# Raw x for the last block's early u, position-major GLU columns, and S4 in the place of S1 with four ev buffers

## The chip, the cores and the metric

The kernel runs on one NeuronCore of a Trainium2 chip. The metric is the device time of one execution in microseconds (us); before the change the median of three runs is 2195.66 us (2195.51 to 2199.68). TensorE (PE) does the matrix products, VectorE (DVE) and ScalarE (ACT) the elementwise work, GpSimd (POOL) a few small powers and some transfers, SyncE (SP) issues most transfers.

## The reference

One decoder layer over 2064 tokens (16 meta tokens ahead of 2048) of width 1024, all in fp32:

```python
hn = rms_norm(h, norm_mix_g)
b_gate, c_gate, v, u = split(hn @ w_in, 4)                 # 512 columns each
conv_out = b_gate * causal_dwconv(c_gate * v, conv_w)
# s5_group_ssm: diagonal complex state space over all tokens, then
g = gelu(Re(C s) + D * u);  ssm_out = g * sigmoid(g @ w_glu)
h = h + concat(rms_norm(conv_out), rms_norm(ssm_out)) @ w_out
hn = rms_norm(h, norm_ffn_g)
a, val = split(causal_dwconv(hn @ w_up, ffn_conv_w, ffn_conv_b))   # 2816 each
h = h + (silu(a) * val) @ w_down
y = rms_norm(h, norm_final_g)[16:]
```

rms_norm multiplies a token by the inverse root mean square over its 1024 features and by a gain g per feature. The inverse root is one number per token, so it can also be multiplied onto a matrix product's output column.

## The kernel before, in words

Features lie on the 128 partitions and tokens along the free dimension. Six chunks of 344 tokens (numbered 0 to 5, q in the code) make three blocks of two chunks. Every fp32 operand is split in a high and a low part, hi = round(x) by ACT and lo = x - hi by DVE; a product is three matmuls with 344 columns, wh times xh, wh times xl, wl times xh. Names with h_ and wh_ are high parts, l_ and wl_ low ones. The weights of a product come by a transfer (wr_), then ACT forms wh_ and DVE wl_.

The stages, in order of time: u and the gated convolution of block 0 (u_block, conv_block; the coefficients of the state space are made on DVE at the same time); the early u of the last block, u_block(2), from about 157 us; u_block(1); conv_block 1 and 2 with the scan of the state space beside them, to about 485 us; the GLU, matmuls pg in glu_block from 505 to 572 us; output projections po to 745 us; then the MLP in three token blocks of some 480 us each. An up product of the MLP is made of two-by-two block products of the weights and of x: seven products (forms) in the place of eight, on sums S1 to S4 of weight blocks, formed on DVE, and on sums of x (t1 to t4 and b21, b22 in the names).

A program written in Python generates the instructions; a scheduler with costs of its own then fixes one order per engine, and each engine works through its order without skipping. Within that, generators (prep) hand out the preparing work of the next chunk in steps between matmul units, and Feed hands out weight splits of the MLP, up to four ahead of use, with three raw weight tiles (tag wr, 3 buffers) in flight.

What the change touches:

- prep_x, as used for chunks 4 and 5, loads the two halves of a chunk, 4 times 344 columns each (x_c), sums the squares (ACT L164 sq_c, DVE adds, PE st_c), forms the inverse root (DVE sv_c, POOL sr_c, DVE dg_c, PE sb_c, ACT rs_c), multiplies it and the gain onto x (DVE L241 t_c, four instructions a half), and only then splits (ACT h_c, DVE l_c). raw_x, used for chunks 0 and 1, splits x times gain at once (ACT L389, DVE L390) and leaves the inverse root to the outputs.
- The halves of x live in a pool with three buffers; a fourth half is loaded when the first has been read for the last time.
- u_block writes a product into ut, transposed to rows of eight positions j, and stores that to u_d (L893). With the inverse root still open this is a DVE multiply (block 0), else an ACT copy (L892).
- After the scan, gt holds g as 4 x 8 x 258 on each partition: feature group k, position j in a group of eight tokens, group c. prep_glu (L1021 and the subtraction behind it) writes gh and gl in token order, with stride 8 across j. glu_block multiplies sg, the sigmoid, onto gt and reads it with stride 8 (tokens()). prep_ssm (from L1033) does the same kind of split for the output projection.
- Pair and PairTile form the weight sums: job 0 splits the raw tile r0 as loaded, then forms three sums in place (S1 in r0's first half, one in its second half, one in the first half of the raw tile r1) and the fourth, S4, in a tile of its own, tag w4, in the pool fp; jobs 1, 2 and 3 split r0 with its sums, S4, and r1. self.freed says at which job a raw tile counts as free for the next load: jobs 1 and 3.
- ev2_tile, the outgoing buffers of the down products (ACT L1525 writes ev, POOL L1529 sends it), has three buffers.

## Time and profile before

| | |
|---|---|
| median of three runs | 2195.66 us (2195.51 to 2199.68) |
| profiled execution, its time | 2199.4 us |
| its span, first to last instruction | 2197.6 us |
| PE busy in the span | 2119.1 us (96%), 13012 matmuls |
| DVE, ACT, POOL busy | 1688.0, 1097.5, 153.2 us |
| mean granted TensorE clock | 0.984 |
| PE idle, 0 to 250 us / 500 to 800 us / 800 to 2197.6 us | 26.7 / 20.0 / 28.2 us |

The span is the stretch from the first to the last instruction of one execution; the profiled one is 3.7 us above the median of the runs. The last row is the window length less PE's busy time in the windows view. A matmul with 344 columns shows about 320 ns in the list, but the next starts while it drains: in stretches without waits one starts each 0.15 to 0.16 us. "Idle before <- X" on a row is the time that the engine stood still ahead of the instruction, and what released it. PEclk is the granted TensorE clock, 1.00 at full speed.

### The profile page before, as it was taken

How to read it: one execution, taken by the hardware profiler on the slowest of the kernel's cores; microseconds unless marked ns; L12 is line 12 of the kernel's file. 1: busy time of each engine (PE TensorE's matmuls, PEld its weight loads, DVE VectorE, ACT ScalarE, POOL GpSimd, SP SyncE). 2: the span in 40 equal slices, each digit the busy share in tenths (PEclk: the TensorE clock that was granted, in tenths of full speed). 3: DMA queues.
4: the chain of work that ended last, by engine and by line, in shares of the span. 5: the costliest groups of instructions: out<-in, count | busy, mean ns of one | idle time of the engine just before them, and what ended most of it. 6: DMA issues, size and time to landing. Idle time of an engine off the chain costs nothing.

```text
span 2197.6 us, 33162 instructions
## 1 busy us (share of the span) xinstructions
PE 2119.1 (96%) x13012; PEld 2057.7 (94%) x13012; DVE 1688.0 (77%) x2539; ACT 1097.5 (50%) x1651; POOL 153.2 (7%) x174
## 2 busy tenths in 40 slices
PE   8997999999899999999999999999999999999997
PEld 7997999998898999999999999999899999999996
DVE  8896498857866796886679878777768878767776
ACT  4135333236523365554556556555456556545555
POOL 0000000000000001101110010100111010110010
PEclk9998999999999999999999999999999999999999
DMA  7376544352475336635552554744554362654463
GB/s 246 104 219 169 142 144 146 116 169 74 144 232 187 100 98 158 157 90 122 133 127 76 144 119 122 184 103 130 147 136 109 103 166 82 163 118 99 98 168 118
DMA packets 170750, 300.29 MB, mean 137 GB/s; under 512 B 32416, under 2 KB 104800, under 8 KB 170464
## 3 DMA queue, kind: packets, MB, share of 16 engines
q1 hardware_dynamic: 149856, 246.41, 36.3%
q0 software_dynamic: 19584, 47.52, 13.0%
q10 hardware_dynamic: 1152, 4.23, 0.5%
q8 instruction: 102, 1.67, 0.3%
q14 instruction: 56, 0.46, 0.1%
HBM read 214.29 MB, written 83.82 MB: 136 GB/s over the span
## 4 chain that ended last, share of the span: by engine, by line
PE 60%; issue 8%; DVE 5%; ACT 3%; DMA 3%; POOL 1%; SPq 0%; POOLq 0%; DVEq 0%; ACTq 0%
PE xy L1427 9%; PE xy L1429 8%; PE xy L1428 8%; PE dn L138 6%; PE dn L139 6%; PE dn L142 6%; PE pz L1429 3%; PE pz L1427 3%; PE pz L1428 3%; PE po L138 2%; PE po L142 2%; PE po L139 1%; DMA v_b<-h_d 1%; DMA gt<-g_d 1%; ACT h_ms L1038 1%
## 5 line engine op out<-in xcount | busy, mean ns | idle before, releaser
L109 DVE TENSOR_TENSOR wl_up<-wr_up,wh_up 128x1024 fp32r<-128x1024 f32 x198 | 241.8, 1222 | 140.7 <-ACT wh_up L248 138.5
L138 PE MATMUL dn<-ah,wh_dn 128*128 128x344 f32 (+1 forms) x1024 | 327.8, 324 | 11.4 <-ACT ah L248 8.8
L139 PE MATMUL dn<-al,wh_dn 128*128 128x344 f32 (+1 forms) x1024 | 325.5, 321 | 0.4 <-DVE al L109 0.3
L248 ACT ACTIVATE wh_up<-wr_up 128x1024 fp32r<-128x1024 f32 x198 | 209.6, 1059 | 230.8 <-PE dn L139 56.4
L1427 PE MATMUL xy<-h_t,wh_up 128*128 128x344 f32 (+1 forms) x792 | 262.8, 332 | 0.0
L1429 PE MATMUL xy<-h_t,wl_up 128*128 128x344 f32 (+1 forms) x792 | 253.4, 320 | 0.0
L1428 PE MATMUL xy<-l_t,wh_up 128*128 128x344 f32 (+1 forms) x792 | 252.7, 319 | 0.0
L142 PE MATMUL dn<-ah,wl_dn 128*128 128x344 f32 (+1 forms) x1024 | 248.1, 321 | 0.0
L138 PEld LDWEIGHTS dn<-ah,wh_dn 128*128 128x128 f32 x1024 | 193.2, 189 | 17.1 <-ACT ah L248 9.7
L1529 POOL DMA_DIRECT2D h_d<-ev x136 | 118.3, 870 | 1261.8 <-ACT ev L1525 1251.4
L139 PEld LDWEIGHTS dn<-al,wh_dn 128*128 128x128 f32 x1024 | 194.2, 190 | 2.0 <-DVE al L109 1.2
L1427 PE MATMUL xy<-h_b,wh_up 128*128 128x344 f32 (+1 forms) x528 | 175.6, 334 | 6.1 <-ACT ev L1525 4.6
L142 PEld LDWEIGHTS dn<-ah,wl_dn 128*128 128x128 f32 x1024 | 178.4, 190 | 0.0
L1428 PE MATMUL xy<-l_b,wh_up 128*128 128x344 f32 (+1 forms) x528 | 169.0, 320 | 0.0
L1429 PE MATMUL xy<-h_b,wl_up 128*128 128x344 f32 (+1 forms) x528 | 167.6, 320 | 0.0
L1427 PEld LDWEIGHTS xy<-h_t,wh_up 128*128 128x128 f32 x792 | 149.2, 188 | 17.1 <-ACT z L1472 11.1
L248 ACT ACTIVATE wh_dn<-wr_dn 128x512 fp32r<-128x512 f32 (+1 forms) x144 | 85.5, 594 | 133.6 <-issue 56.7
L1428 PEld LDWEIGHTS xy<-l_t,wh_up 128*128 128x128 f32 x792 | 149.9, 189 | 0.0
L1429 PEld LDWEIGHTS xy<-h_t,wl_up 128*128 128x128 f32 x792 | 149.6, 189 | 0.0
L115 DVE SCALAR_TENSOR_TENSOR g<-z,pv,g 128x688 f32<-128x688 f32 (+1 forms) x132 | 122.3, 926 | 23.7 <-ACT g L1432 22.9
L115 DVE SCALAR_TENSOR_TENSOR v<-z,pneg,v 128x688 f32<-128x688 f32 (+1 forms) x132 | 122.4, 927 | 10.3 <-ACT v L1432 9.0
L109 DVE TENSOR_TENSOR wl_dn<-wr_dn,wh_dn 128x512 fp32r<-128x512 f32 (+1 forms) x144 | 92.3, 644 | 45.6 <-ACT wh_dn L248 44.9
(413 smaller groups left out, 5358.3 us busy)
## 6 DMA issues: line engine op xcount, KB each, us to landing
wr_up<-in_w_up SPq DMA_DIRECT2D x132, 512.0 KB, 5.0
h_d<-ev POOLq DMA_DIRECT2D x88, 344.0 KB, 6.6
wr_dn<-in_w_down SPq DMA_DIRECT2D x96, 256.0 KB, 2.6
wr_cw<-in_w_in SPq DMA_DIRECT2D x36, 512.0 KB, 4.6
h_d<-ev POOLq DMA_DIRECT2D x48, 336.0 KB, 6.7
x_c<-in_xq SPq DMA_DIRECT2D x16, 688.0 KB, 6.4
wr_dn<-in_w_down SPq DMA_DIRECT2D x48, 192.0 KB, 2.3
xr<-in_xq SPq DMA_DIRECT2D x24, 344.0 KB, 3.7
```

The source lines that it names most:

```text
L109: V.tensor_tensor(out, a, b, op=op)
L115: V.scalar_tensor_tensor(out=out, in0=a, scalar=s, in1=b, op0=ALU.mult, op1=ALU.add)
L138: T.matmul(ps[c], hi[:, k, :], xh, start=k == 0, stop=False)
L139: T.matmul(ps[c], hi[:, k, :], xl, start=False, stop=False)
L142: T.matmul(ps[c], lo[:, k, :], xh, start=False, stop=k == nk - 1)
L248: S.activation(hi, t, AF.Copy)
L1038: S.activation(tokens(hi), t, AF.Copy)
L1427: T.matmul(ps, hi[:, j, :], xh[:, j, :], start=start and j == 0, stop=False, **kw)
L1428: T.matmul(ps, hi[:, j, :], xl[:, j, :], start=False, stop=False, **kw)
L1429: T.matmul(ps, lo[:, j, :], xh[:, j, :], start=False, stop=j == 3, **kw)
L1529: G.dma_start(out=h_d[:, m, s0 : s0 + no], in_=ev, accum_op=ALU.add)
```

## The change

Three edits, and their names. First, chunks 4 and 5 go through raw_x for the early u of the last block: they are split without the inverse root, x of chunk 4 is loaded ahead of conv_block(0), the inverse root is kept in rs_2 (the same single buffer as that of block 0), and ut is then written by a DVE multiply. Second, prep_glu writes gh and gl by position (j c) and no longer by token, and glu_block reads sg in runs of 43. Third, in the MLP S4 is formed in the first half of r0, where S1 lay, after S1's split; r0 counts as free after job 2 instead of job 1; the tile w4 goes; ev2 gets a fourth buffer.

```diff
-    rs0 = rs_tile("rs0")[:, :, :QL]
+    rs_of = {}
-    def raw_x(q, res):
+    def raw_x(q, res, b, other=False, late=None):
         xs, out = [], []
+        kw = dict(pool=xf2, tag="xhl2", bufs=4) if other else {}
         for i in range(2):
             xs += load_halves((xq[q, :, 4 * i : 4 * i + 4, :],), QL, f"c{q}{i}")
             yield
-        for i, x in enumerate(xs):
-            hi, lo = hl_tile(QL, f"h_c{q}_{i}"), hl_tile(QL, f"l_c{q}_{i}")
+        def split_half(i, x):
+            hi, lo = hl_tile(QL, f"h_c{q}_{i}", **kw), hl_tile(QL, f"l_c{q}_{i}", **kw)
             for k in range(4):
                 g = col(C_MIX + 4 * i + k)
                 S.activation(hi[:, k, :], x[:, k, :], AF.Copy, scale=g)
...
-        yield from inv_rms(xs, QL, f"c{q}", rs0[:, q, :])
+        for i, x in enumerate(xs):
+            if late is None:
+                split_half(i, x)
+            else:
+                late.append(lambda x=x, i=i: split_half(i, x))
+            yield
+        if b not in rs_of:
+            rs_of[b] = rs_tile(f"rs_{b}")[:, :, :QL]
+        yield from inv_rms(xs, QL, f"c{q}", rs_of[b][:, q % 2, :])
...
-                prep.add(prep_x(4, hu, other=True), prep_x(5, hu, late=late))
+                prep.add(ahead[0], raw_x(5, hu, 2, late=late))
...
-            if b == 0:
-                mul(out, by_j(ps[:, :, :QL]), by_j(rs0))
+            if b in rs_of:
+                mul(out, by_j(ps[:, :, :QL]), by_j(rs_of[b]))
...
     u_block(0, hc[0])
+    ahead = [raw_x(4, hu, 2, other=True)]
+    next(ahead[0])
+    next(ahead[0])
     conv_block(0, hc[0], late_after=True, n_prep=4)
...
-            S.activation(tokens(hi), src, AF.Copy)
-            tt(tokens(lo), src, f32(tokens(hi)), ALU.subtract)
+            hj, lj = (a.rearrange("p k (j c) -> p k j c", j=NJ) for a in (hi, lo))
+            S.activation(hj, src, AF.Copy)
+            tt(lj, src, f32(hj), ALU.subtract)
...
-            g = gt[:, m, :, b * 86 : b * 86 + 86]
-            mul(g, g, tokens(sg))
+            g = gt[:, m, :, b * 86 : b * 86 + 86].rearrange("p j (c x) -> p c j x", c=2)
+            mul(g, g, two(sg).rearrange("p c (j x) -> p c j x", j=NJ))
...
-            self.freed = int(i in (1, 3))
+            self.freed = int(i > 1)
...
-                pair.s4 = fp.tile([P, 4, P], F32, tag="w4", bufs=1, name=f"w4_{pair.name}")
-                tt(pair.s4, r1[:, 4:8, :], b, ALU.add)
                 return w
-            return split_weights((r0, pair.s4, r1)[i - 1], 4 if i == 2 else 8, f"{pair.name}_{i}")
+            if i == 2:
+                return split_weights(a, 4, f"{pair.name}_2")
+            w = split_weights(r0 if i == 1 else r1, 8, f"{pair.name}_{i}")
+            if i == 1:
+                tt(a, r1[:, 4:8, :], b, ALU.add)
+            return w
...
-        return fp.tile([P, MAX_OUT], F32, tag="ev2", bufs=3, name=name)
+        return fp.tile([P, MAX_OUT], F32, tag="ev2", bufs=4, name=name)
```

The rows below are single instructions in the order in which an engine works through them: line, operation, output <- inputs with buffer numbers, columns on each partition, and xN for N like rows in a row. Line numbers are those of each version. In the GLU the order is the same in both; only the shapes differ.

DVE ahead of the early u of the last block (chunk 5: sv_c5 and dg_c5 are steps of its inverse root, t_c5 the normed x, l_c5 its low part, tab and wr, wi tables of the state space). Before:

```order
L198 TENSOR_SCALAR sv_c5_1652<-st_c5_1648 115x3
L109 TENSOR_TENSOR wi_0_2577<-tab_coarse_1320,tab_fine_1293 128x544
L203 TENSOR_SCALAR dg_c5_1656<-ident_75,sr_c5_1653 115x115 x2
L109 TENSOR_TENSOR st_0_2575<-wr_0_2576,wi_0_2577 128x544
L203 TENSOR_SCALAR dg_c5_1656<-ident_75,sr_c5_1653 115x115
L801 MEMSET sb_0_2755 128x4
L241 SCALAR_TENSOR_TENSOR t_c5_0_1729<-x_c5_0_1580,pv_84,rs_c5_1662 128x344 x4
L241 SCALAR_TENSOR_TENSOR t_c5_1_1734<-x_c5_1_1582,pv_84,rs_c5_1662 128x344 x4
L109 TENSOR_TENSOR l_c5_0_1795<-t_c5_0_1729,h_c5_0_1794 128x4x344
L109 TENSOR_TENSOR l_c5_1_1799<-t_c5_1_1734,h_c5_1_1798 128x4x344
```

Now, ending with the same sv_c5:

```order
L394 SCALAR_TENSOR_TENSOR l_c4_1_1428<-x_c41_0_659,pv_84,h_c4_1_1427 128x344 x4
L109 TENSOR_TENSOR tc_0_3_1725<-tc_0_3_1725,rs_0_184 128x688
L394 SCALAR_TENSOR_TENSOR l_c5_0_1786<-x_c50_0_1525,pv_84,h_c5_0_1785 128x344 x2
L109 TENSOR_TENSOR tc_0_3_1725<-cb_0_3_1730,tc_0_3_1725 128x688
L109 TENSOR_TENSOR wl_u22_1809<-wr_u22_1598,wh_u22_1808 128x1024
L109 TENSOR_TENSOR wl_u23_1886<-wr_u23_1670,wh_u23_1885 128x1024
L109 TENSOR_TENSOR sq_c5_0_1586<-sq_c5_0_1586,sq_c5_1_1588 128x4x344
L394 SCALAR_TENSOR_TENSOR l_c5_1_1796<-x_c51_0_1584,pv_84,h_c5_1_1795 128x344
L109 TENSOR_TENSOR sq_c5_0_1586<-sq_c5_0_1586 128x2x344
```

The low part of chunk 5 stood behind the inverse root of chunk 5 and now stands ahead of it.

DVE at the start of the MLP (up0_0 is the first pair of weight tiles; _2 is S4's split, _3 that of r1; po_2_7 is the last product of the output projection, xr its sum with x, l_b and l_t low parts of the MLP's x). Before:

```order
L109 TENSOR_TENSOR xr_2_7_6599<-po_2_7_6734,xr_2_7_6599 128x688
L109 TENSOR_TENSOR l_b22_0_6790<-v_b22_0_6585,h_b22_0_6789 128x4x338
L109 TENSOR_TENSOR l_b21_0_6794<-v_b21_0_6586,h_b21_0_6793 128x4x338
L109 TENSOR_TENSOR l_t3_0_6799<-v_b12_0_6584,h_t3_0_6798 128x4x338
L1217 TENSOR_SCALAR pneg_6814<-pv_84 128x22 x3
L109 TENSOR_TENSOR w4_up0_0_6829<-wr_up0_0_1_6820,wr_up0_0_0_6818 128x512
L109 TENSOR_TENSOR wl_up0_0_2_6836<-w4_up0_0_6829,wh_up0_0_2_6835 128x512
L109 TENSOR_TENSOR wl_up0_0_3_6840<-wr_up0_0_1_6820,wh_up0_0_3_6839 128x1024
```

Now:

```order
L109 TENSOR_TENSOR l_t4_0_6734<-v_b11_0_6586,h_t4_0_6733 128x4x338
L109 TENSOR_TENSOR wr_up0_0_0_6821<-wr_up0_0_1_6823,wr_up0_0_0_6821 128x512
L109 TENSOR_TENSOR wl_up0_0_2_6838<-wr_up0_0_0_6821,wh_up0_0_2_6837 128x512
L109 TENSOR_TENSOR xr_2_7_6602<-po_2_7_6737,xr_2_7_6602 128x688
L109 TENSOR_TENSOR l_b22_0_6793<-v_b22_0_6588,h_b22_0_6792 128x4x338
L109 TENSOR_TENSOR wl_up0_0_3_6842<-wr_up0_0_1_6823,wh_up0_0_3_6841 128x1024
L109 TENSOR_TENSOR l_b21_0_6797<-v_b21_0_6589,h_b21_0_6796 128x4x338
L109 TENSOR_TENSOR l_t3_0_6802<-v_b12_0_6587,h_t3_0_6801 128x4x338
```

S4's sum and split moved ahead of the last xr, and r1's split ahead of l_b21.

DVE at the change from the second to the third token block of the MLP (v_b11 to v_b22 are quarters of the next x, scaled by its inverse root rsk; up1_16 is a pair of weight tiles). Before:

```order
L1143 SCALAR_TENSOR_TENSOR v_b11_2_15387<-v_b11_2_15387,pv_84,rsk_2_13516 128x344 x2
L1143 SCALAR_TENSOR_TENSOR v_b21_2_15390<-v_b21_2_15390,pv_84,rsk_2_13516 128x344 x3
L109 TENSOR_TENSOR wl_up1_16_0_14829<-wr_up1_16_0_14715,wh_up1_16_0_14828 128x1024
L1143 SCALAR_TENSOR_TENSOR v_b12_2_15388<-v_b12_2_15388,pv_84,rsk_2_13516 128x344
L109 TENSOR_TENSOR wr_up1_16_0_14715<-wr_up1_16_0_14715,wr_up1_16_1_14762 128x512
```

Now:

```order
L1160 SCALAR_TENSOR_TENSOR v_b11_2_15349<-v_b11_2_15349,pv_84,rsk_2_13486 128x344 x3
L109 TENSOR_TENSOR wl_up1_16_0_14794<-wr_up1_16_0_14680,wh_up1_16_0_14793 128x1024
L1160 SCALAR_TENSOR_TENSOR v_b12_2_15350<-v_b12_2_15350,pv_84,rsk_2_13486 128x344
L109 TENSOR_TENSOR wr_up1_16_0_14680<-wr_up1_16_0_14680,wr_up1_16_1_14727 128x512
L1160 SCALAR_TENSOR_TENSOR v_b12_2_15350<-v_b12_2_15350,pv_84,rsk_2_13486 128x344
```

v_b21, the quarter that is loaded last, stood ahead of that pair's first split; now the first v_b21 stands thirteen rows behind it, ahead of S4's split.

More of the change, by code (lines that the diff above doesn't have):

```diff
@@ L384, in raw_x @@
             yield
-        for i, x in enumerate(xs):
-            hi, lo = hl_tile(QL, f"h_c{q}_{i}"), hl_tile(QL, f"l_c{q}_{i}")
+        if other:
+            kw["pool"] = xf2
+        def split_half(i, x):
+            hi, lo = hl_tile(QL, f"h_c{q}_{i}", **kw), hl_tile(QL, f"l_c{q}_{i}", **kw)
             for k in range(4):
@@ L393, in raw_x @@
             out.append((hi, lo))
+            if i == 1:
+                res.append(out)
+        for i, x in enumerate(xs):
[3 more added lines that the diff above has]
+                late.append(lambda x=x, i=i: split_half(i, x))
             yield
-        res.append(out)
-        yield from inv_rms(xs, QL, f"c{q}", rs0[:, q, :])
+        if b not in rs_of:
+            rs_of[b] = rs_tile(f"rs_{b}")[:, :, :QL]
+        yield from inv_rms(xs, QL, f"c{q}", rs_of[b][:, q % 2, :])
     sgn = col(C_SGN)
@@ L902, in conv_block @@
             if b == 0:
-                mul(two(vs), pv_[:, :, :QL], rs0)
+                mul(two(vs), pv_[:, :, :QL], rs_of[0])
             else:
@@ L910, in conv_block @@
             if b == 0:
-                mul(two(vs), two(vs), rs0)
+                mul(two(vs), two(vs), rs_of[0])
             tt(two(cv[:, 2:]), pc[:, :, :QL], two(vs), ALU.mult)
@@ L918, in conv_block @@
             if b == 0:
-                mul(two(tp), two(tp), rs0)
+                mul(two(tp), two(tp), rs_of[0])
             after_unit(n_prep=n_prep)
@@ L969, in layer_kernel @@
     hu, late = [], []
-    first = [raw_x(q, hc[0]) for q in range(2)]
+    first = [raw_x(q, hc[0], 0) for q in range(2)]
     next(first[0])
@@ L1320, in split @@
                 tt(b, b, a, ALU.add)
-                pair.s4 = fp.tile([P, 4, P], F32, tag="w4", bufs=1, name=f"w4_{pair.name}")
-                tt(pair.s4, r1[:, 4:8, :], b, ALU.add)
-                return w
-            return split_weights((r0, pair.s4, r1)[i - 1], 4 if i == 2 else 8, f"{pair.name}_{i}")
+                return w
+            if i == 2:
+                return split_weights(a, 4, f"{pair.name}_2")
+            w = split_weights(r0 if i == 1 else r1, 8, f"{pair.name}_{i}")
+            if i == 1:
+                tt(a, r1[:, 4:8, :], b, ALU.add)
+            return w
     jobs = []
```

## The prediction

> **What bounds the kernel now.** The page's first part and the windows view (columns: stretch, length, then busy time of each engine with its instructions in brackets, granted TensorE clock, DMA share, GB/s) come first.
>
> ```profile
> PE 2119.1 (96%) x13012; PEld 2057.7 (94%) x13012; DVE 1688.0 (77%) x2539; ACT 1097.5 (50%) x1651; POOL 153.2 (7%) x174
> 150.00:200.00 50.00, 38.90 (x224) 36.69 (x223) 37.95 (x55) 24.30 (x22) 2.04 (x2) 0.86 0.69 198
> 200.00:250.00 50.00, 46.47 (x292) 45.18 (x291) 20.05 (x27) 21.93 (x19) 1.50 (x2) 1.00 0.64 152
> 500.00:550.00 50.00, 45.10 (x254) 43.53 (x253) 43.21 (x50) 33.94 (x36) 3.20 (x3) 0.90 0.20 59
> 550.00:600.00 50.00, 44.35 (x264) 42.71 (x263) 44.01 (x62) 26.98 (x26) 3.10 (x3) 0.93 0.44 130
> 800.00:1050.00 250.00, 249.70 (x1581) 243.44 (x1581) 192.85 (x263) 136.94 (x219) 22.88 (x26) 1.00 0.50 124
> ```
>
> PE is busy 96% of the span, and no matmul is added or taken away, so only its waits and its half-clock stretches can be won. In 800 to 1050 us it is full: 250 us for 1581 matmuls, 0.158 us each. Counted so, 150 to 250 us holds 516 matmuls, 81.5 us of work, and 18.5 us are lost; 500 to 600 holds 518, 81.8 us, and 18.2 are lost. Those are the first two edits' stages. The third edit works in the MLP, where most windows are like the last row: there it can win little and lose much.
>
> **Part A, x of the last block without its inverse root.** The timeline of PE between 160 and 216 us shows the chain that u_block(2) waits for, then u_block(1); last the window with the half clock, and the DVE rows of the second chain.
>
> ```profile
> 164.82 0.76 PE L188 MATMUL st_c<-ones,sq_c 128*115 128x1 f32 x6 [3.33 <-DVE sq_c L109]
> 168.50 0.94 PE L208 MATMUL sb_c<-dg_c,ones 115*128 115x344 f32 x1 [2.92 <-DVE dg_c L203]
> 174.02 0.65 PE L138 MATMUL pu<-h_c,wh_u 128*128 128x344 f32 x1 [4.00 <-ACT h_c L248]
> 174.00:179.50 5.50, 4.63 (x15) 4.19 (x16) 4.08 (x5) 4.06 (x3) 0.00 (x0) 0.50 0.74 249
> 202.20 1.59 DVE L109 TENSOR_TENSOR sq_c<-sq_c,sq_c 128x1376 f32<-128x1376 f32 x1 [2.04 <-ACT sq_c L164]
> 213.48 3.10 DVE L109 TENSOR_TENSOR l_c<-t_c,h_c 128x1376 fp32r<-128x1376 f32 x2
> 215.12 0.43 PE L139 MATMUL pu<-l_c,wh_u 128*128 128x344 f32 x1 [1.34 <-DVE l_c L109]
> ```
>
> The edit takes the inverse root of chunks 4 and 5 off the path to their matmuls: these now need only the split. Removed on DVE are 16 t_c (L241) and four l_c of 1376 columns; added are 16 raw splits (L390's kind) and four ut multiplies in the place of ACT's copies. Per tile, DVE and ACT:
>
> ```profile
> L241 DVE SCALAR_TENSOR_TENSOR t_c<-x_c,pv,rs_c 128x344 f32<-128x344 f32 x48 | 24.0, 571 | 2.9 <-ACT rs_c L213 2.9
> L390 DVE SCALAR_TENSOR_TENSOR l_c<-x_c,pv,h_c 128x344 fp32r<-128x344 f32 x16 | 8.5, 572 | 5.9 <-ACT h_c L389 5.9
> L109 DVE TENSOR_TENSOR l_c<-t_c,h_c 128x1376 fp32r<-128x1376 f32 x12 | 18.7, 1589 | 0.0
> L109 DVE TENSOR_TENSOR ut<-pu,rs x4: 1450/1494/1534, 37.4 to 48.9; 128x688 f32<-128x688 f32 x4
> x_c<-in_xq SPq DMA_DIRECT2D x16, 688.0 KB, 6.4
> ```
>
> DVE does 16 x 0.57 + 4 x 1.59 = 15.5 us less and 16 x 0.57 + 4 x 1.49 = 15.1 more: nothing on balance; ACT gives up the four ut copies and forms h_c of chunks 4 and 5 in 16 pieces in the place of four, on an engine that is busy 24.30 and 21.93 us of 50 in the two windows above: nothing. What counts is the order. Followed by hand with these durations, PE goes on at once behind conv_block(0), where before it stood 3.33 + 2.92 + 4.00 us and ran at 0.50 until 179.5. One wait stays: the second half of chunk 5 gets its buffer only when chunk 4's first half is split, and the transfer takes 6.4 us; I get 2 us of PE idle (0 if it is issued early, 5 at twice the queue).
>
> That does not carry through to the end of u_block(1). Chunk 3's x is still normed first, and its second half needs a buffer that chunk 2's t_c gives back. The row at 202.20 starts its sum of squares and the one at 213.48 its low part: from 202.20 to the end of the first l_c, 213.48 + 1.55 = 215.0, are 12.8 us, a chain of DVE, PE, POOL and ACT that the edit leaves alone. In the new order t_c of chunk 2 comes about 6 us sooner, so this chain ends near 209, while PE would be there near 197. PE stands some 10 us in u_block(1), and the gain of about 19 us (the 18.5 lost plus rounding) shrinks to 215 - 209 = 6. From this I take 1 us for a half-clock stretch behind the new stand, as at 174 us. **A: 5 us won**; bounds 0 (chunk 3 no sooner than before) and 14 (its load lands early, and 18.5 less the waits left, 2 us and their half clock, is won).
>
> **Part B, the GLU's columns by position.** The view of tile gt (columns: minimum, median and maximum ns, first and last start), the group of the contiguous split of the conv half (l_mc), and the stage's PE rows:
>
> ```profile
> L109 DVE TENSOR_TENSOR gt<-gt,sg x12: 1395/1508/1556, 521.4 to 573.3; 128x688 f32<-128x688 f32 x12
> L1021 ACT ACTIVATE gh<-gt x6: 2768/2951/3092, 497.6 to 515.0; 128x1376 fp32r<-128x1376 f32 x6
> L109 DVE TENSOR_TENSOR gl<-gt,gh x6: 2754/2944/3064, 500.6 to 518.1; 128x1376 fp32r<-128x1376 f32 x6
> L164 ACT ACTIVATE sq_ms<-gt x6: 1355/1366/1382, 529.1 to 652.5; 128x1376 f32<-128x1376 f32 x6
> L109 DVE TENSOR_TENSOR l_mc<-t_mc,h_mc 128x1376 fp32r<-128x1376 f32 x6 | 9.4, 1590 | 0.1
> 562.01 0.86 DVE L109 TENSOR_TENSOR sq_mc<-sq_mc 128x688 f32<-128x688 f32 x1
> 507.51 0.65 PE L142 MATMUL pg<-gh,wl_g 128*128 128x344 f32 x1 [2.26 <-DVE wl_g L109]
> 534.60 0.42 PE L188 MATMUL st_ms<-ones,sq_ms 128*115 128x1 f32 x2 [1.79 <-DVE sq_ms L109]
> 564.04 0.32 PE L188 MATMUL st_mc<-ones,sq_mc 128*115 128x1 f32 x1 [4.87 <-DVE sq_mc L109]
> 534.50:542.00 7.50, 7.40 (x29) 7.43 (x30) 4.69 (x10) 0.76 (x1) 2.03 (x2) 0.54 0.26 72
> 504.80:564.00 59.20, 49.47 (x279) 47.61 (x278) 52.66 (x61) 39.91 (x40) 3.20 (x3) 0.90 0.18 51
> ```
>
> sq_ms reads gt in the same runs of 43 as gh and gl will, and takes 1.37 us; the strided writes take 2.95 for as many columns. So gh goes to 1.37, gl to 1.59, and the gate multiply, 688 columns, from 1.51 to the 0.86 of the row at 562.01. Nothing is added. DVE, the engine that PE waits for, is relieved ahead of st_mc by 6 x 1.35 = 8.1 us and nine of the twelve multiplies, 9 x 0.65 = 5.9, together 14.0; ACT by 6 x 1.58 = 9.5, all ahead of the first sigmoid. From 504.8, the first pg matmul, to st_mc PE takes 59.2 us for 279 matmuls (the last row), 44.1 us at 0.158, so 15.1 could be won at most. By hand, with the unchanged order, the waits at 507.51 and 534.60 and their slow stretches vanish, but st_mc still waits about 4 us: t_ms, both l_ms (still strided) and t_mc stand ahead of it on DVE. It comes at 552.7 in the place of 564.04. **B: 11 us won**, bounds 7 (only the two first waits and the half of the slow 7.5 us at 534.5, 2.26 + 1.79 + 3.5, rounded down) and 15.1.
>
> A rule of the Trainium skill bears on the 2 us wait of part A: TensorE: Matmul & The Clock Gate, section "Part 1: The HAM clock gate", has the clock halve only after an idle window of about 3.4 us. By it that wait would be free of a slow stretch, and the sum of A 1 to 2 us better. Here a wait of 1.79 us (the row at 534.60) is followed by 7.5 us at 0.54; the trace disagrees, and I go by it.
>
> On reads in runs of odd length the Trainium skill has a price: Vector Engine (DVE) Microarchitecture Reference, section "5.2 Measured stream behaviour on trn2", gives 1.30 ns for a column in the place of 1.05 where adjacent words start on an odd word, and every second run of 43 does. By that page gl would take 1.86 us and the multiply 0.97 (estimates), 2.9 us over all, and B would win 8 to 9. sq_ms, on the other engine, shows no such extra.
>
> **Part C, S4 in S1's place, four ev buffers.** Three rows of PE with what DVE and ACT did ahead of them, and the MLP's weight loads:
>
> ```profile
> 754.58 0.43 PE L1427 MATMUL pz<-h_b,wh_up 128*128 128x338 f32 x1 [1.59 <-ACT wh_up L248]
> 755.00:760.00 5.00, 4.64 (x21) 4.46 (x20) 4.69 (x6) 1.50 (x4) 0.00 (x0) 0.66 0.48 160
> 752.23 0.68 DVE L109 TENSOR_TENSOR w_up<-wr_up,wr_up 128x512 f32<-128x512 f32 x1
> 1554.64 1.55 DVE L1143 SCALAR_TENSOR_TENSOR v_b<-v_b,pv,rsk 128x344 f32<-128x344 f32 x3 [6.30 <-DMA v_b<-h_d]
> 1561.60 0.73 ACT L1525 ACTIVATE ev<-dn 128x688 f32<-128x688 f32 x1
> 1562.38 0.65 PE L1427 MATMUL xy<-h_b,wh_up 128*128 128x344 f32 x1 [4.60 <-ACT ev L1525]
> 959.00 1.22 DVE L109 TENSOR_TENSOR wl_up<-wr_up,wh_up 128x1024 fp32r<-128x1024 f32 x1
> 960.14 0.68 DVE L109 TENSOR_TENSOR wl_up<-w_up,wh_up 128x512 fp32r<-128x512 f32 x1
> 967.91 0.68 DVE L109 TENSOR_TENSOR wr_up<-wr_up,wr_up 128x512 f32<-128x512 f32 x1
> wr_up<-in_w_up SPq DMA_DIRECT2D x132, 512.0 KB, 5.0
> ```
>
> Operations and their sizes stay. At the start, S4 waited at 752.23 for the pool fp to open; without w4 its sum and split fit ahead of the last xr, in DVE's idle time. PE's 1.59 us and most of the slow stretch to 760 go: 3 us. At 1562.38 the named release, ev, is late only since DVE stood 6.30 us for the quarter v_b21 ahead of the split of the pair 16; ACT queued behind with the pair's wh, and ev behind that. In the new order that split precedes v_b21: 4.60 us and half of a slow stretch, 5 us (bounds 0, if the quarter that now precedes it is as late, and 6). The fourth ev buffer ends ACT's waits for transfers; only one PE wait of 1.2 us names ev elsewhere, and I give it nothing. Against this, r0 is freed by the split at 960.14 and no longer by that at 959.00: 1.1 us later, and the load of the next tile, SP's queue behind it, with it. Issued at 960.8 it lands near 966, ahead of the sum at 967.91; with 5.0 us to land 2 us of slack remain. PE is a form of 12 matmuls or more behind, so I charge 1 us in all. **C: 7 us won**, bounds 10 won and 6 lost (0.1 us in each of 66 pairs, beyond which the slower rival begins).
>
> **The sum.** 5 + 11 + 7 = 23 us: the span goes from 2197.6 to 2174.6, with 1.8 us around it 2176.4 against 2199.4. The profiled execution is 3.7 us above the median; taken from 2195.7, the forecast is 2173.
>
> **Rivals.** (1) A gives nothing: chunk 3 is loaded behind chunk 5's tail and its chain ends as late as before, 215. For it speaks that three buffers tie each load to the half three ahead; against it that t_c of chunk 2 no longer stands behind eight t_c of chunk 5. 2195.7 - 18 = 2178. (2) A gives nearly all, 14: chunk 3's load lands while PE is in u_block(2). The same three buffers speak against it. 2195.7 - 32 = 2164. (3) B's DVE part fails: reads in runs of 43 at fp32 cost what stride 8 cost. sq_ms speaks against it, but that is ACT. ACT's 9.5 us and gl's contiguous write remain, B wins about 4: 2180. (4) Slower: the later release of r0 stalls the MLP. In each of the 66 pairs the next load comes 1.1 us later; where it misses the sum, DVE waits in order, and with it the additions that empty PSUM. DVE is at 77% there, so up to some slack it catches up, and the full PE windows speak against it; from 23/66 = 0.35 us a pair on it eats the whole gain. At half of 1.1 us, 0.55 x 66 = 36 us lost: 2209.
>
> **Chances.** Forecast 0.55, (1) 0.17, (2) 0.12, (3) 0.07, (4) 0.09. For the range, 2160 to 2189: its low end is (2) with C at its bound, its high end A at 0, B at 7 and C at 0; the forecast's own range is 2166 to 2181. A measurement of this kernel can tell 0.2%, 4.4 us, from no change. Faster holds in all cases but (4), and there milder forms land between: faster 0.87, same 0.05, slower 0.08.
>
> **What would show it.** Right for A: no wait for h_c of chunk 5 behind conv_block(0), and one long wait for l_c in u_block(1). Right for B: gh at 1.4, gl at 1.6, multiplies at 0.9 us, no wait at the start of pg, and st_mc still waiting some 4 us. Right for C: 750 to 760 with some 60 matmuls, no wait of 4.6 us at the block change, and MLP windows as full as that of 800 to 1050. Wrong would be waits of PE on wh_up or ev spread over the pairs, or gl still near 3 us.

## The result

The changed kernel takes 2182.45 us (median of four, 2177.14 to 2185.18), the kernel before 2195.59 us: the ratio of the runs is 0.9935, 95% interval 0.9911 to 0.9958. That is 14 us faster by the ratio (9 to 20), where 23 were forecast; 2182 lies in the range of 2160 to 2189, but above the forecast's own 2166 to 2181. The profiled execution took 2185.18 us with a span of 2183.3, so the two profiled spans differ by 14.3 us.

A median hides where that comes from. The table gives, for the same instruction in both traces (the last ut eviction, the last sigmoid of the GLU, the last xr sum, then evictions of the MLP that do not change places), its start in the changed kernel less its start in the kernel before.

| Place, start before (us) | after - before (us) | forecast |
|---|---|---|
| end of u_block(1), 242 | -4.9 | -5 |
| end of the GLU, 573 | -15.2 | -16 |
| end of the output projections, 746 | -16.0 | -16 |
| MLP, first block, 791 | -20.3 | -19 |
| MLP, ahead of the third block, 1498 | -18.0 | -19 |
| behind its beginning, 1604 | -17.3 | -24 |
| MLP, near its end, 2146 | -15.4 | -23 |
| span | -14.3 | -23 |

Parts A and B came as forecast. Part C won at the start of the MLP and nothing at the change of blocks, and lost some 4 us bit by bit over the pairs (2.3 us from 791 to 1498 and 1.9 from 1604 to 2146).

The windows view of the changed kernel (stretch, length, busy time with instructions of PE, PEld, DVE, ACT, POOL, granted clock, DMA share, GB/s):

```profile
150.00:200.00 50.00, 46.47 (x292) 44.89 (x290) 45.15 (x70) 25.21 (x33) 3.53 (x3) 0.99 0.87 243
200.00:250.00 50.00, 44.55 (x258) 43.10 (x259) 17.27 (x25) 17.50 (x15) 0.85 (x1) 0.87 0.55 138
500.00:550.00 50.00, 45.64 (x287) 44.55 (x286) 39.63 (x59) 31.52 (x37) 2.95 (x3) 0.97 0.23 69
550.00:600.00 50.00, 47.52 (x284) 45.88 (x284) 42.16 (x63) 22.41 (x22) 3.09 (x3) 0.96 0.64 205
750.00:800.00 50.00, 50.00 (x316) 48.66 (x316) 47.47 (x65) 32.77 (x55) 0.00 (x0) 1.00 0.34 102
800.00:1050.00 250.00, 249.66 (x1578) 242.91 (x1578) 186.77 (x257) 135.88 (x219) 25.92 (x29) 1.00 0.51 126
1550.00:1600.00 50.00, 50.00 (x308) 48.22 (x308) 38.32 (x51) 29.05 (x54) 2.59 (x3) 1.00 0.33 84
```

150 to 200 us now holds 292 matmuls in the place of 224, but 200 to 250 only 258 in the place of 292: the loss moved on a stage. The GLU's two windows hold 571 in the place of 518. And 800 to 1050 is as full as before, with 1578 records against 1581: the loss in the MLP does not show as idle time of PE.

The waits that remain, from PE's timeline of the changed kernel, and the clock behind two of them:

```profile
197.77 0.76 PE L188 MATMUL st_c<-ones,sq_c 128*115 128x1 f32 x6 [1.15 <-DVE sq_c L109]
200.60 1.52 PE L208 MATMUL sb_c<-dg_c,ones 115*128 115x344 f32 x2 [2.06 <-DVE dg_c L203]
206.12 1.23 PE L138 MATMUL pu<-h_c,wh_u 128*128 128x344 f32 x3 [4.00 <-ACT h_c L248]
206.00:212.00 6.00, 5.03 (x16) 4.60 (x17) 4.58 (x5) 4.13 (x4) 0.00 (x0) 0.50 0.73 231
548.37 0.32 PE L188 MATMUL st_mc<-ones,sq_mc 128*115 128x1 f32 x1 [4.36 <-DVE sq_mc L109]
548.00:556.00 8.00, 7.63 (x34) 7.66 (x35) 5.63 (x11) 1.26 (x2) 1.16 (x1) 0.62 0.46 152
1537.81 0.65 PE L138 MATMUL dn<-ah,wh_dn 128*128 128x344 f32 x1 [3.90 <-ACT ev L1545]
```

The first three are the chain of chunk 3 in u_block(1), the one that the forecast had PE run into; the fifth is the wait for sq_mc that the forecast left standing; the last is the change of blocks, which the forecast had emptied. ACT there, at the same time:

```profile
1536.07 1.06 ACT L248 ACTIVATE wh_up<-wr_up 128x1024 fp32r<-128x1024 f32 x1 [7.20 <-DMA wr_up<-in_w_up]
1537.03 0.72 ACT L1545 ACTIVATE ev<-dn 128x688 f32<-128x688 f32 x1
```

DVE no longer stands for v_b21. Now ACT stands 7.20 us for the first weight tile of pair 16, and ev, for which PE waits, is behind it in ACT's order. That tile was issued at 1522.77 and landed at 1535.96, 13.2 us, where the profile's page gives 4.9 for the median of all such loads; between 1516 and 1530 all four quarters of v_b, four ev stores and three weight tiles are in the queues, and the DMA share of 1520 to 1545 us is 0.98. Behind the wait the clock is 0.57 from 1537.8 to 1545 us.

### The profile page after: what moved, and what is told of

It is laid out like the page before. It is cut to its first block, busy times and chain, and to the rows that moved or that the text cites. A ratio compares the mean times of both kernels' runs of the same rounds, so it can differ in the third digit from the quotient of the medians.

```text
span 2183.3 us, 33128 instructions
## 1 busy us (share of the span) xinstructions
PE 2117.2 (97%) x13012; PEld 2055.2 (94%) x13012; DVE 1666.3 (76%) x2539; ACT 1087.4 (50%) x1659; POOL 153.5 (7%) x174
## 4 chain that ended last, share of the span: by engine, by line
PE 69%; DVE 5%; DMA 2%; ACT 1%; issue 1%; POOLq 0%; DVEq 0%; SPq 0%; ACTq 0%
PE xy L1447 10%; PE xy L1449 9%; PE xy L1448 9%; PE dn L138 7%; PE dn L139 7%; PE dn L142 7%; PE pz L1449 4%; PE pz L1448 4%; PE pz L1447 4%; PE po L138 2%; PE po L142 2%; PE po L139 2%; DMA wr_up<-in_w_up 1%; PE pg L138 1%; PE pg L139 1%
## 5 line engine op out<-in xcount | busy, mean ns | idle before, releaser
L109 DVE TENSOR_TENSOR wl_up<-wr_up,wh_up 128x1024 fp32r<-128x1024 f32 (+1 forms) x264 | 286.3, 1089 | 172.6 <-ACT wh_up L248 172.6
L248 ACT ACTIVATE wh_up<-wr_up 128x1024 fp32r<-128x1024 f32 (+1 forms) x264 | 247.5, 950 | 288.9 <-DVE wr_up L109 95.6
L109 DVE TENSOR_TENSOR wr_up<-wr_up,wr_up 128x512 f32<-128x512 f32 x198 | 136.3, 689 | 8.1 <-DMA wr_up<-in_w_up 5.3
```

The source lines that it names most:

```text
L109: V.tensor_tensor(out, a, b, op=op)
L248: S.activation(hi, t, AF.Copy)
```

## The experiments

Each kernel was run beside the kernel before on the same chip; ratios are to those runs. Traces are compared by the starts of the same evictions, as in the table above.

**e1, e2: parts A and B alone.** The edits are the hunks of the change up to conv_block, and those of prep_glu and glu_block.

> The kernel before with part A alone (raw x for chunks 4 and 5). Theory: the parts are independent, since each acts in its own stage; A alone wins the 4.9 us that the change had gained by the end of u_block(1), so about 2190.7, with PE's wait of some 8 us for chunk 3 in u_block(1) as in the changed kernel and the GLU and MLP as before. Rival: A's gain is used up by the GLU's transfers or by later waits, and the time is within 1 us of before; or A's earlier loads help the stages behind and it wins 7 or more.

> The kernel before with part B alone (GLU columns by position). Theory: it wins the 10.3 us of the changed kernel's trace by the end of the GLU and a further 0.8 in the output projections, about 2184.5; the MLP's start as before. Rival: part of those 10 us needed A's or C's order, and B alone wins 7 or less.

A alone: 2191.66 us, ratio 0.9964 (0.9946 to 0.9982); its trace is 3.7 us ahead at the end of u_block(1), 4.4 at the end of the GLU and 7.5 at 746. Of those last 3.1 us some 1.6 also come in e5 and e6 below, which run the order of the kernel before. B alone: 2186.02 us, ratio 0.9939 (0.9924 to 0.9954); its trace starts 1.8 us late and gains 10.6 by the last sigmoid and 1.0 more by 746. In its own stage each does alone about what it did in the change. By the ratios A and B together make 0.990, more than the whole change with 0.9935. The intervals still meet, so this is only a sign that something in part C costs time; e3 tests it.

**e3, e4: part C without the fourth buffer.** e3 is the kernel before with S4 in S1's place, e4 the changed kernel with three ev buffers. The fourth buffer alone cannot be tried: with w4 still there the pool of the MLP does not fit in SBUF, so the two edits of part C belong together.

```diff
-        return fp.tile([P, MAX_OUT], F32, tag="ev2", bufs=4, name=name)
+        return fp.tile([P, MAX_OUT], F32, tag="ev2", bufs=3, name=name)
```

> The kernel before with S4 in S1's place and its later release, but three ev buffers. Theory: 4 us won at the start of the MLP, nothing at the change of token blocks near 1560 us (there the wait goes from the quarter v_b21 to the pair's late first weight tile), and some 3 us lost bit by bit over the pairs, since ACT's split of S4 now waits for DVE: 2194 to 2195. Rival 1: the bit by bit loss is chance between executions; then 2191. Rival 2: the late weight tile at the block change comes of the fourth ev buffer's transfers; then that wait is gone here and the time is about 2187.

> The changed kernel with three ev buffers in the place of four. Theory: the fourth buffer does nothing that PE feels, 2182 to 2183. Rival 1: its transfers crowd the queues at the block change, and with three the wait of 3.9 us on ev near 1538 goes: 2178. Rival 2: with three buffers ACT's waits for transfers return and PE feels them: 2185 or more.

e3: 2201.68 us, ratio 1.0020 (1.0010 to 1.0030), slower than before by 2 to 7 us. e4: 2183.05 us, ratio 0.9924 (0.9902 to 0.9947), not to be told from the change. So the fourth buffer does nothing that the times can tell, and S4's place costs time. One place differs in the traces: at the change of blocks PE waits 1.6 us in e4 and 3.9 in the change, and e4's trace gains 3 us there. In e3, with three buffers as well, PE waits 3.4 us there, so this is not shown to be the buffer's doing. Part C was forecast to win 7 us. e3 was expected to be some 1 us faster than the kernel before; by the ratio it is 4.4 us slower. The trace of e3 shows a gain at the start of the MLP (3.0 us ahead at 791) and then a loss that never stops: 1.2 ahead at 1498, 3.6 behind at 2146.

What differs in the MLP of e3 is seen in the waits of ACT and of PE's weight loads between 800 and 2100 us (columns: sum, times, longest). The kernel before, then e3:

```profile
ACT wh_up L248 <- DVE wr_up L109: 45.7, 35, 7.5
ACT g L1432 <- DVE z L109: 12.1, 13, 1.9
PEld xy L1427 <- DVE z L109: 3.6, 20, 0.2
```

```profile
ACT wh_up L248 <- DVE wr_up L109: 88.2, 61, 3.3
ACT g L1435 <- DVE z L109: 35.7, 39, 2.2
PEld xy L1430 <- DVE z L109: 5.7, 32, 0.2
```

ACT waits almost twice as long for DVE's weight sums, and the weight loads of xy wait more often for DVE to empty PSUM, at most 0.2 us at a time. Two things in the edit could do this: the raw tile r0 is given back later (the forecast's slower rival), or S4's sum can no longer be formed ahead of S1's split, since it overwrites S1.

**e5, e6: the two causes apart, first attempt.** On the kernel before, e5 only counts r0 free at job 2, e6 only forms S4's sum (in its own tile) behind the split of S1:

```diff
-            self.freed = int(i in (1, 3))
+            self.freed = int(i > 1)
```

```diff
                 tt(b, b, a, ALU.add)
-                pair.s4 = fp.tile([P, 4, P], F32, tag="w4", bufs=1, name=f"w4_{pair.name}")
-                tt(pair.s4, r1[:, 4:8, :], b, ALU.add)
                 return w
...
+            if i == 1:
+                pair.s4 = fp.tile([P, 4, P], F32, tag="w4", bufs=1, name=f"w4_{pair.name}")
+                tt(pair.s4, r1[:, 4:8, :], b, ALU.add)
+            return w
```

> The kernel before, S4 in its own tile and formed with the other sums as before, but r0 counted free at job 2 (one line). It asks what the slow loss over the MLP's pairs in the S4-in-place kernels comes from (6.6 us from the first pair to the last in the trace of S4 alone). Theory 1, S4's sum now stands between the splits of S1 and S4 and ACT waits for it: the loss is absent here, 2196 to 2199, as before. Theory 2 (the prediction's), the next tile's load is late: the loss is here, 2203 or more.

> The kernel before with S4 in its own tile w4 and r0 counted free at job 1, but S4's sum formed behind the split of S1, as in the change. Theory 1 (ACT's split of S4 waits for the late sum, and PSUM is emptied later behind it): 6 to 7 us lost over the pairs, 2203 to 2205. Theory 2 (the late load): no loss, 2196 to 2199.

2197.92 us, ratio 1.0000 (0.9990 to 1.0009), and 2197.52, ratio 0.9998 (0.9986 to 1.0009). Neither loses anything, but neither tests anything either. The scheduler gave every engine of e5 exactly the order of before, and in e6 it put the sum back ahead of the split, since nothing forbids it. On DVE, for one pair of e6 (rows of other tiles left out), S4's sum, S1's split, S4's split:

```
L109 TENSOR_TENSOR w4_up1_5_12443<-wr_up1_5_1_12322,wr_up1_5_0_12269 128x512
L109 TENSOR_TENSOR wl_up1_5_1_12440<-wr_up1_5_0_12269,wh_up1_5_1_12439 128x1024
L109 TENSOR_TENSOR wl_up1_5_2_12481<-w4_up1_5_12443,wh_up1_5_2_12480 128x512
```

What the two do give is the spread of nearly one and the same order: their traces end 3.3 and 6.2 us ahead of that of before, so a few microseconds between two single traces mean little, and only drifts that several traces share are read below.

**e9, e10: the two causes forced.** A dependence that the scheduler must keep takes the place of an order in the program. e9 copies one column of r0's second half onto itself behind S1's split; S4's sum, still in its own tile, reads that half and so cannot go ahead of the split. e10 keeps the early sum and, behind S4's split, adds one column of that split into r0, so r0's buffer is really held until then.

```diff
+            if i == 1:
+                V.tensor_copy(b[:, 0, 0:1], b[:, 0, 0:1])
+                pair.s4 = fp.tile([P, 4, P], F32, tag="w4", bufs=1, name=f"w4_{pair.name}")
+                tt(pair.s4, r1[:, 4:8, :], b, ALU.add)
```

```diff
+            if i == 2:
+                tt(r0[:, 0, 0:1], f32(w[1][:, 0, 0:1]), r0[:, 0, 0:1], ALU.add)
```

> In e5 and e6 the scheduler had given every engine the same order as before, so they changed nothing that runs. Here the kernel before gets, behind S1's split, a DVE copy of one column of r0's second half onto itself, and S4's sum (still into its own tile) reads that half: the sum cannot go ahead of S1's split. Theory 1 (ACT's split of S4 waits for the sum): ACT's waits for DVE's weight sums grow from 45 to some 85 us between 800 and 2100 us, and 5 to 7 us are lost bit by bit over the MLP: ratio 1.002 to 1.003, less about 0.1 us x 66 for the copies if DVE feels them. Theory 2 (the later release of r0): no creeping loss beyond what the copies cost.

> The kernel before with S4's early sum in its own tile, and behind S4's split a DVE add of one column that reads that split and writes into r0: r0's buffer is really given back only then, as in the change, while ACT never waits longer. Theory 2 (late release, the prediction's slower rival): the creeping loss of 5 to 7 us is here, ratio 1.002 to 1.003. Theory 1: ratio 1.000, ACT's waits for the sums stay near 45 us, at most 1 us of creep.

e9: 2209.60 us, ratio 1.0050 (1.0034 to 1.0065). e10: 2199.51 us, ratio 1.0007 (0.9997 to 1.0017). With the late sum and its copies 7 to 14 us are lost; with the late release nothing that can be told from zero, though its interval reaches 3.7 us. Both dependences hold, as the pairs between 800 and 2100 us show. The times count from the start of S1's split; the load is taken in the 42 to 44 pairs in which it leaves within 10 us, since in the others it leaves 20 us later in every kernel.

| kernel | next raw tile's load issued (us): median, lowest to highest | S4's split ends (us): median |
|---|---|---|
| before | 1.25, 1.24 to 1.26 | 2.24 |
| after | 3.82, 3.37 to 4.69 | 3.81 |
| e3 | 3.83, 3.37 to 4.68 | 3.83 |
| e9 | 2.50, 2.20 to 3.58 | 4.25 |
| e10 | 3.80, 2.08 to 4.24 | 2.24 |

So e10 gives r0 back late in every pair (2.0 us later than the kernel before on the mean, where the change is 2.6 later), with S4's split as early as before.

The waits between 800 and 2100 us of e9, then of e10:

```profile
ACT wh_up L248 <- DVE wr_up L109: 55.8, 38, 5.8
ACT wh_up L248 <- DVE w_up L109: 10.0, 11, 1.7
ACT v L1435 <- DVE z L109: 31.5, 18, 1.9
PEld xy L1430 <- DVE z L109: 8.4, 48, 0.2
PEld pz L1430 <- ACT wh_up L248: 7.5, 17, 0.8
```

```profile
ACT wh_up L248 <- DVE wr_up L109: 55.6, 40, 7.4
PEld xy L1430 <- DVE z L109: 3.6, 20, 0.2
```

The expectation of 85 us for ACT's waits in e9 was wrong: 55.8 and 10.0 for its sums, and instead ACT waits for z. So was that of 45 us in e10, 55.6, so this row does not tell the two apart. The row on xy does: 48 waits of the weight loads for DVE's z in e9, 32 in e3, 20 in e10 and before. It is a mark and not the price of the loss, for its sum grows by only 2.1 us in e3, and all waits of xy's weight loads together are 27.5 us in e3 and 32.1 in e10. What decides is the drift of the traces, in two stretches of the MLP that leave out the change from the second to the third block:

| kernel | S4's sum | 791 to 1498 (us) | 1604 to 2146 (us) |
|---|---|---|---|
| e1, e2 | early, own tile | +0.8, -1.7 | +0.4, +0.5 |
| e5, e6 | early, own tile | -1.6, -3.2 | -1.1, 0.0 |
| e10 | early, r0 held | +1.2 | -0.5 |
| after | late, in place | +2.3 | +1.9 |
| e3, e4 | late, in place | +1.8, +2.0 | +4.5, +2.7 |
| e9 | late, own tile | +4.3 | +3.9 |

All are against the trace of before. Added over the two stretches, the lowest loss with the late sum is 4.2 us, the highest without it 1.2. It is clearest where no trace jumps, from 1224 to 1497 us (the first and last eviction of pz there): the nine kernels with the early sum, e7, e8, e11 and e12 below among them, move by 0.2 us at most, the four with the late one lose 0.9 to 1.6. That e9 loses more than e3 goes with its 66 added copies of 0.15 us, each between a split and a sum on DVE; how much of its loss is theirs was not tried. An added instruction of that length is not enough by itself, since e10 has one in each pair as well.

**e7: S4 in place for the first pair alone.** Parts A and B, and of part C what won: the first pair of the MLP has no tile w4 to wait for, all other pairs keep the early sum; there are three ev buffers.

```diff
+            self.in_place = b == f == 0
...
-            self.freed = int(i in (1, 3))
+            self.freed = int(i > 1 if pair.in_place else i in (1, 3))
```

> Parts A and B, with S4 in S1's place in the first pair of the first token block only, and S4 in w4 with its early sum in the other 65 pairs; three ev buffers. Theory: A, B and the gain of 4 to 5 us at the start of the MLP stay, and the slow loss over the pairs goes: 2175 to 2178 against 2198, ratio near 0.990, faster than the change by 5 us or more. Rival: the slow loss comes of the MLP's earlier start (a different phase of transfers), and the time is that of the change, 2182.

2178.21 us (2176.99 to 2178.82), ratio 0.9907 (0.9892 to 0.9922). Its trace drifts by -1.9 and +0.4 us in the two stretches of the table, like those of the kernels without part C. The gain at the start stays (-17.8 at 746, -21.3 at 791; without C the traces of e1, e2, e5 and e6 move by -1.3 or -1.4 there, so some 2 to 3 us are C's). It is 4 us faster than the change by the medians; the ratios' intervals overlap.

**e8: raw x for chunks 2 and 3 too.** On e7, block 1 goes through raw_x as well, and u and the convolution of block 1 get their inverse root on DVE as in block 0 (the second part of the cut stands at three places):

```diff
-    prep.add(prep_x(2, hc[1]), prep_x(3, hc[1], other=True, late=late))
+    prep.add(raw_x(2, hc[1], 1), raw_x(3, hc[1], 1, other=True, late=late))
...
-            if b == 0:
+            if b < 2:
```

> The kernel of e7 with raw x for chunks 2 and 3 too (block 1; u and the convolution of block 1 then get their inverse root by DVE multiplies, as in block 0). Theory: PE's wait of 8 us in u_block(1) was the norm of chunk 3 ahead of its split, so that wait and its half-clock stretch go, 8 to 10 us less than e7 by 250 us; DVE's added multiplies in conv_block(1) (12 of 0.87 us in the place of four copies on ACT) are hidden: 2167 to 2170. Rival 1: the wait is for chunk 3's load, which needs a buffer that chunk 2 gives back, and most of it stays: 2174 or more. Rival 2: DVE, 81% busy in the convolutions, gives the gain back there: 2175 or more.

2172.20 us (2170.98 to 2173.58), ratio 0.9881 (0.9866 to 0.9896). Its windows:

```profile
150.00:200.00 50.00, 47.96 (x301) 46.30 (x300) 44.50 (x73) 31.95 (x49) 3.95 (x3) 1.00 0.96 260
200.00:250.00 50.00, 50.00 (x316) 49.77 (x315) 25.57 (x33) 10.76 (x13) 1.41 (x1) 1.00 0.58 155
```

The wait in u_block(1) is gone, down to 0.69 us for st_c and 0.85 for sb_c, and with it the half clock: the last ut comes 14.8 us ahead of before where e7's came 3.8 ahead, 11 us. By the first sigmoid of the GLU the gain over e7 is 8.6, so the convolutions with DVE's added multiplies took back 2.4. The norm of chunk 3 ahead of its split was the bound. Raw x also reads each half sooner, so its buffers come free sooner, but by the traces the load alone would have been in time. In the changed kernel the second half of chunk 3 had landed at 189.29 us, e8 splits both halves of that chunk within 6.4 us (188.27 to 194.64), and PE's first wait began only at 196.62. How much of the 11 us the earlier loads add was not taken apart.

**e11: t_ms in token order.** On e8, the strided step moves from ACT's h_ms and DVE's l_ms to DVE's t_ms:

```diff
-                out=t[:, k], in0=src[:, k], scalar=col(C_GS + k), in1=rs.rearrange("p (j c) -> p j c", j=NJ),
+                out=tokens(t)[:, k], in0=src[:, k], scalar=col(C_GS + k), in1=rs.rearrange("p (j c) -> p j c", j=NJ),
...
-        S.activation(tokens(hi), t, AF.Copy)
-        tt(tokens(lo), t, f32(tokens(hi)), ALU.subtract)
+        S.activation(hi, t, AF.Copy)
+        tt(lo, t, f32(hi), ALU.subtract)
```

> The kernel of e8, with the normed GLU output t_ms written in token order (four strided DVE writes of 344 columns) so that h_ms and l_ms are contiguous. It tests what the 4 us wait of PE for sq_mc is made of. Theory (the strided l_ms ahead of it on DVE): the two l_ms lose 1.4 us each, and the wait shrinks by what the eight strided t_ms do not give back: if a strided write costs 0.33 us more for 344 columns, DVE is even, the wait stays at 3 to 4 us and the time within 2 us of e8. Rival: strided writes cost nothing for instructions so short, and the wait falls to about 1.5 us, 2169.

2162.32 us (2157.15 to 2162.97), ratio 0.9827 (0.9808 to 0.9847): the fastest kernel of the study, 20 us ahead of the change and 10 ahead of e8. The view of tile t_ms in e8, and in e11 (minimum, median, maximum ns), each followed by the two l_ms ahead of sq_mc and PE's wait for sq_mc:

```profile
L1050 DVE SCALAR_TENSOR_TENSOR t_ms<-gt,pv,rs_ms x24: 568/572/579, 523.2 to 656.2; 128x344 f32<-128x344 f32 x24
L1055 ACT ACTIVATE h_ms<-t_ms x6: 2860/2991/3101, 527.0 to 657.4; 128x1376 fp32r<-128x1376 f32 x6
L109 DVE TENSOR_TENSOR l_ms<-t_ms,h_ms x6: 2935/2971/3134, 530.0 to 660.5; 128x1376 fp32r<-128x1376 f32 x6
529.99 6.18 DVE L109 TENSOR_TENSOR l_ms<-t_ms,h_ms 128x1376 fp32r<-128x1376 f32 x2 [0.94 <-ACT h_ms L1055]
540.84 0.90 PE L188 MATMUL st_mc<-ones,sq_mc 128*115 128x1 f32 x4 [4.22 <-DVE sq_mc L109]
```

```profile
L1050 DVE SCALAR_TENSOR_TENSOR t_ms<-gt,pv,rs_ms x24: 829/888/927, 523.1 to 650.8; 128x344 f32<-128x344 f32 x24
L1055 ACT ACTIVATE h_ms<-t_ms x6: 1344/1360/1368, 526.9 to 651.7; 128x1376 fp32r<-128x1376 f32 x6
L109 DVE TENSOR_TENSOR l_ms<-t_ms,h_ms x6: 1591/1597/1618, 530.2 to 653.1; 128x1376 fp32r<-128x1376 f32 x6
530.15 3.19 DVE L109 TENSOR_TENSOR l_ms<-t_ms,h_ms 128x1376 fp32r<-128x1376 f32 x2
538.04 0.33 PE L188 MATMUL st_mc<-ones,sq_mc 128*115 128x1 f32 x2 [1.32 <-DVE sq_mc L109]
```

By the lengths of the records DVE would be even (four t_ms at 0.316 us more are 1.26, one l_ms 1.37 less), and yet PE's wait for sq_mc falls from 4.22 to 1.32 us. But the records overlap: each t_ms starts 0.49 us behind the one before it in e8 and 0.69 in e11, 0.20 more and not 0.32. From the first t_ms to the end of the two l_ms DVE takes 12.83 us in e8 (523.18 to 536.01) and 10.18 in e11. Of the 2.65 us between them 1.16 are DVE's own work (11.33 us busy, then 10.17). The other 1.50 are waits that are gone: 1.05 for h_ms, which is 1.63 us shorter on ACT and stands in the chain between t_ms and l_ms, and 0.45 for the statistics product sb_ms. So the theory that DVE's own work sets this wait holds for less than half of it, and the rival's price, strided writes that cost nothing, is wrong as well. By the traces e11 is 4.3 us ahead of e8 at the end of the GLU and 6.4 at the end of the output projections (the spans differ by 8.3), where e8's waits of 1.86 us for xr and 1.23 for h_ms are gone or cut to 0.45.

**e12: v_b21 loaded second.** On e8, in the second and third block of the MLP:

```diff
         load("b11", 0, 0)
+        if b:
+            load("b21", 1, 0)
         load("b12", 0, 1)
         load("b22", 1, 1)
-        load("b21", 1, 0)
+        if not b:
+            load("b21", 1, 0)
```

> The kernel of e8, with the quarter v_b21 of the second and third MLP block loaded second in the place of last. Theory 1: at the change from the second to the third block the transfer of v_b21, for which DVE stands ahead of the first split of pair 16, is the late one; loaded second it is there, the wait of 4 to 5 us near 1531 and its half-clock stretch go, 2166 to 2168. Theory 2 (as in the changed kernel, where the wait moved to pair 16's first weight tile, 13 us on its way): so much is in the queues there that another transfer is late in its place; the wait stays within 2 us, and the time is that of e8, 2171 to 2174.

2167.27 us, ratio 0.9855 (0.9839 to 0.9871). PE's wait at the change of blocks:

```profile
1530.99 0.42 PE L1453 MATMUL xy<-h_b,wh_up 128*128 128x344 f32 x1 [2.82 <-ACT ev L1551]
```

2.82 us in the place of 4.83 in e8, and across the place its trace gains 3.1 us on that of e8. By the times, 2167 us against 2172, the two ratios' intervals just meet. Neither theory holds whole: the late quarter was part of it, and with it out of the way ev is still late. What the rest is made of stays open; e11 and e12 together were not run.

## Why the prediction was right or wrong

**A, 5 us: right, by the chain forecast.** 4.9 us by the trace, 8 us by e1's ratio (4 to 12). PE went on at once behind conv_block(0). The 2 us wait for chunk 5's second half did not come (the waits there add up to 0.9 us), so the question of what the clock does behind such a wait was not put there. The row that the prediction cites for it, 1.79 us at 534.60, has twelve matmuls of one column around it, with 3.4 us between the full matmuls on either side; the cleaner case in the same trace is the wait of 2.26 us at 507.51, full matmuls on both sides, with a clock of 0.53 from 507.5 to 511. The stand in u_block(1) is 1.15 + 2.06 + 4.00 + 0.84 = 8.1 us and not 10; but the half clock behind it costs more than the 1 us charged: from 206 to 212 us the clock was 0.50, and half of the 5.03 us that PE is busy there is 2.5 us. The two misses nearly cancel, so that the size came out so close is partly luck; the mechanism is not. e8 shows the cause as forecast, the norm of chunk 3.

**B, 11 us: right.** 10.3 us by the last sigmoid and 0.8 more in the output projections. The instructions measure as the rows of other engines and shapes had said:

```profile
L109 DVE TENSOR_TENSOR gt<-gt,sg x12: 849/875/883, 507.0 to 558.1; 128x688 f32<-128x688 f32 x12
L1038 ACT ACTIVATE gh<-gt x6: 1353/1362/1367, 492.7 to 503.0; 128x1376 fp32r<-128x1376 f32 x6
L109 DVE TENSOR_TENSOR gl<-gt,gh x6: 1584/1586/1595, 494.1 to 504.4; 128x1376 fp32r<-128x1376 f32 x6
```

1.36, 1.59 and 0.88 us against 1.37, 1.59 and 0.86 forecast. Reading in runs of 43 costs DVE nothing, where the price taken from the Trainium skill (Vector Engine (DVE) Microarchitecture Reference, section 5.2) would have made gl 1.86. That estimate also charged too much: it took the price for all columns, while gt's rows are 258 wide, so that its runs start on an odd word in every second chunk only, and gl's other operand is contiguous. The six gl differ by 11 ns at most. The wait for sq_mc stayed at 4.36 us, forecast 4; that it was a matter of DVE's own work alone is what e11 refuted.

**C, 7 us: wrong, and here the 9 us between forecast and result lie.** Its terms one by one. The start of the MLP, 3 us: right (4.3 by the trace, some 3 against kernels without C, e1, e2, e5 and e6, whose traces gain 1.3 or 1.4 on that of before there). The change of blocks, 5 us: measured nothing (0.7 us lost by the trace). The reasoning about v_b21 was right, and its wait did go; the bound given for it named only the quarter that comes next, not the weight tile that shares the queues, and that tile was 13.2 us on its way. "DVE stood ahead of the split" was one of two transfers that were late at once. The charge for the pairs, 1 us: measured 4 to 6 us, near the forecast's bound of 0.1 us in each of 66 pairs. The step that failed there is the mechanism: the part costed the later release of r0, and passed over the dependence that the new place creates. S4's sum now overwrites S1, so it must follow S1's split, ACT's split of S4 must follow the sum, and S4's split ends 1.6 us later in each pair (3.81 us behind the start of S1's split in the place of 2.24). With it r0 came free 2.6 us later and not 1.1, but e10, where it comes free 2.0 us later with the early sum, loses nothing that can be told from zero. How the late split turns into PE's loss is argued and not shown: behind it in their orders stands DVE's and ACT's work that empties PSUM. "Operations and their sizes stay" was true, and not enough.

The rivals: (4) had the right sign for part C and the right place, pairs one after the other, but the wrong cause and 9 times the price (36 us against some 4). (1), (2) and (3) did not happen: A won 4.9 us, and gl and the multiply fell as forecast, though the number alone, 2182, lies closer to (3), 2180, than to the forecast's 2173.

## What to carry to other kernels

Forming a result in the place of an operand saves a buffer and adds an order: whoever read the old content must be done first. Look at which engine waits for that reader, even where no operation is added. When a wait has been taken off, ask which chain is next in the same stage, and cost that one before the sum is made; and where a scheduler fixes the order, moving code tests nothing until a dependence holds it, so compare the orders before spending a run.

## What the runs showed of the hardware

Stride 8 in fp32 costs time for each column. By the lengths of the records it is 0.92 ns more on DVE with one strided output (t_ms, 0.888 against 0.572 us for 344 columns), 0.92 with one strided input (the gate multiply, 1.508 against 0.875 for 688), and 1.00 with a strided input and output together (l_ms, 2.97 against 1.60 for 1376). Where like instructions follow each other their records overlap, and by the distance of their starts the strided output of t_ms costs less, 0.6 ns a column (0.69 against 0.49 us). So it paid to move the stride from two instructions, on two engines, to one. And a loss of 4 us and more over the MLP came with PE shown as busy in its windows; it was found in the starts of the evictions, compared between traces.
